# Where the buffers live in SBUF: TensorE's operands stacked from the low end, raw weights, h and small pieces from the high end

## The chip, the cores and the metric

One core of a Trainium2 chip runs the whole program. The metric is the device time of one execution in microseconds (us). Runs of one kernel repeat within some tenths of a microsecond here; of a change in this kernel a measurement can tell about 0.2%.

## What is computed

One layer of a streaming encoder on 256 tokens of width 2048, in float32:

```python
h = x + 0.5 * swiglu(rms_norm(x), ffn1...)             # d_ff = 5632
u = rms_norm(h); z_pool, q, k, v = split(u @ w_in)     # w_in 2048 x 4096
y_pool = pool_mixer(z_pool)                            # 4 groups, windows 2, 4, 8, 16
y_attn = chunk_attention(q, k, v)                      # 8 heads of 128, chunk 64
gates = sigmoid(u @ w_branch_gate + b)                 # 2048 x 4096
merged = gates_pool * (y_pool @ w_br_pool) + gates_attn * (y_attn @ w_br_attn)
h = h + merged @ w_out
h = h + 0.5 * swiglu(rms_norm(h), ffn2...)
h = h + sigmoid(rms_norm(h) @ w_ple_gate) * (p @ w_ple)
```

The inputs hold 444 MB of data that the DMAs move, nearly all of it weights that are read once.

## The kernel before

**Weights in two words.** Every weight tile, 512 rows by 512 columns (128 partitions x 4 x 512, 8 KB per partition), comes as float32 by one DMA into a raw buffer (`wraw`). ScalarE rounds it to a float32r high word `whi` (L155), VectorE subtracts for the low word `wlo` (L163). TensorE's left-hand operands (the activations, turned so that tokens are columns) are split in the same way, by `split` (L112 to L114). A product then has three passes per 128 rows: low activation x `whi` (L198), high activation x `whi` (L200), high activation x `wlo` (L205). In each, the 128x128 activation tile is loaded into the array and 512 columns of the weight tile stream past it. Each of the three lines issues 2,884 matmuls of that shape.

**Items.** The program is a flat list of items (one weight tile and its matmuls), which `stream` (L172) writes out: for item i it issues the DMAs of up to five items ahead (as rooms are free), the high word of item i + 2, the low word of item i + 1 and the matmuls of item i. Engine queues are in the order in which this writes them (`manual_schedule`). Four of the six raw buffers are not interchangeable: `ROOMS` (L38) gives one each to the tags wa, wb, wc, and three to wr.

**Blocks.** The FFN products and the last gate use `block` (L375), which makes 2x2 tiles of four weights with seven products instead of eight: seven items of 12 matmuls, and two or four "rest" items of 24 matmuls on the inner tiles beyond the first 1024 (L423). Three sums of raw weights are made in the raw buffers by VectorE (L413, L417, L420) and one by an accumulating DMA of GpSimd (L414). An FFN runs in parts of 4, 4 and 3 column blocks (`FFN_PARTS`, L37); each part has its up/gate blocks, whose left-hand operands are the normed `u` tiles (`uah`, `ual`, `ush`, `usl`, `uhi`, `ulo`), and two down blocks, whose left-hand operands are the `hid` tiles. A down block has two rest items per side in parts 1 and 2 and one per side in part 3.

**Mixer.** Between the FFNs, `mixer` (L750) computes the input projection, attention, pooling, the gates (`w_branch_gate`), and per 512 columns `w_br_pool` and `w_br_attn` of 8 tiles' depth, in two items each: the first on `ypool` (kept in the room wc) or on spare `u` tiles, the second on `ypoolhi`/`ypoollo` or `yattnhi`/`yattnlo` of the pool `mix`. Of the four `merged` operands that `w_out` reads, the first two lie in the rooms wa and wb, the other two (`mergedl`) in `mix`. `v` and `z` lie in wa and wb too.

**Homes.** A pool is a run of addresses, the same on all partitions; pools are stacked in the order in which they are opened. Homes in KB of a partition, as built:

| what | before | changed |
|---|---|---|
| `ident` and other constants (pool const) | 16 to 17 | 16 to 17 |
| raw weights, tag wr (3) | 17 to 41 | 176 to 200 |
| `whi` (3) | 41 to 65 | 17 to 41 |
| `wlo` (2) | 65 to 81 | 41 to 57 |
| rooms wa, wb, wc (raw weights; `merged`, `v`, `z`, `ypool`) | 81 to 105 | 200 to 224 |
| `h` (2) | 105 to 121 | 149 to 165 |
| `u` tiles (pool act) | 121 to 165 | 57 to 101 |
| small pieces, statistics (pool work) | 165 to 176 | 165 to 176 |
| pools hid, mix, late, opened and closed on the way | 176 to 224 | 101 to 149 |

Of the kernel before, what the change touches and what calls it, by code (L numbers as in the profile page):

```python
# [10 lines left out]
F32 = mybir.dt.float32  # L11
F32R = mybir.dt.float32r
# [4 lines left out]
P = 128  # L17
SEQ = 256
NT = SEQ // P
D = 2048  # L20
# [13 lines left out]
NB = 512  # L34
KB = 4
KW = 2
FFN_PARTS = (4, 4, 3)  # L37
ROOMS = {"wa": 1, "wb": 1, "wc": 1, "wr": 3}  # L38
# [3 lines left out]
def hybrid_block(ctx: ExitStack, tc: tile.TileContext, a: dict, out: bass.AP):  # L42
    nc = tc.nc

    const = ctx.enter_context(tc.tile_pool(name="const", bufs=1))
    wpool = ctx.enter_context(tc.tile_pool(name="wpool", bufs=1))
    act = ctx.enter_context(tc.tile_pool(name="act", bufs=1))
    work = ctx.enter_context(tc.tile_pool(name="work", bufs=1))
    ps_acc = ctx.enter_context(tc.tile_pool(name="ps_acc", bufs=6, space=bass.MemoryType.PSUM))
    ps_tp = ctx.enter_context(tc.tile_pool(name="ps_tp", bufs=2, space=bass.MemoryType.PSUM))  # L50

# [34 lines left out]
    def piece_tile(name):  # L86
        return work.tile([P, NB], F32, tag="piece", name=name, bufs=PIECES)
# [11 lines left out]
    def later(steps, task):  # L99
        waiting.append([steps, task])  # L100
# [18 lines left out]
    def room(tag, name):  # L119
        assert free[tag] > 0, tag  # L120
        free[tag] -= 1
        return wpool.tile([P, KB, NB], F32, tag=tag, name=name, bufs=ROOMS[tag])

    class Weight:

# [5 lines left out]
        def load(self):  # L131
            self.raw = room(self.tag, "wraw")
            at_once = KW if self.halves else self.nk
            for k in range(0, self.nk, at_once):
                ks = slice(k, k + at_once)
                nc.sync.dma_start(self.raw[:, ks, :], self.src[:, ks, :])
# [109 lines left out]
    def product(w, lhs, n0, done, k0=0, nks=(KB,) * (D // P // KB), halves=False):  # L246

        got = []

        def banks():  # L250
            if not got:
                got.extend(acc_tile("acc") for _ in range(NT))
            return got

        items, kt = [], k0
        for i, nk in enumerate(nks):
            end = i == len(nks) - 1
            items.append(Item(
                Weight(w, kt, n0, nk, halves=halves and not i),
                both(banks, lambda i=i: lhs()[i], done if end else None, last=end),  # L260
            ))
            kt += nk
        return items
# [204 lines left out]
        nc.vector.tensor_tensor(r, r, s, op=ALU.mult)  # L468
        return r

    h = [act.tile([P, D], F32, tag=f"h{t}", name=f"h{t}") for t in range(NT)]

    def token_tiles(b):

# [8 lines left out]
    def turn(dst, src, t):  # L483

        tp = turned(src)
        if isinstance(dst, Half) and not dst.b:
            f = dst.place(t)
            nc.scalar.copy(out=f, in_=tp)
            dst.take(t, f)
        else:  # L490
            dst.take(t, tp)
# [120 lines left out]
    def hooked(items, before):  # L612

        mm = items[0].mm

        def new(it):
            before()
            mm(it)

        items[0].mm = new  # L620
        return items
# [128 lines left out]
    def mixer(norm, following, flat, carry):  # L750
# [7 lines left out]

        def begin():
            mix = m_["mix"] = inner.enter_context(tc.tile_pool(name="mix", bufs=1))  # L760
            yp = wpool.tile([P, 2, KB, SEQ], F32R, tag="wc", name="ypool", bufs=ROOMS["wc"])
            free["wc"] -= 1
            y["pool"] = [
                Operand(None, "", 1, missing=KB, tiles=(yp[:, 0], yp[:, 1])),
                Operand(mix, "ypool", 1, missing=KB),
            ]

            yh, yl = (s[:, 2:4, :].rearrange("p b (k s) -> p (b k) s", s=SEQ) for s in norm.spare)
            y["attn"] = [
                Operand(None, "", 1, missing=KB, tiles=(yh, yl)),  # L770
                Operand(mix, "yattn", 1, missing=KB),
            ]
# [50 lines left out]
        for blk in range(2):  # L823
            for which, c0 in (("q", POOL_W), ("k", POOL_W + 1024)):
                items = product(w_in, lhs, c0 + blk * NB, heads(which))
                if first:
                    hooked(items, begin)
                    first = False
                flat += items


        def plain(c0, tag, name, then):
            got = []
            items = []
            for blk in range(2):
                def done(accs, blk=blk):
                    if not got:
                        both_ = room(tag, name)
                        got.extend(both_[:, 2 * t:2 * t + 2, :] for t in range(NT))
                    for t in range(NT):  # L840
                        nc.scalar.activation(got[t][:, blk, :], accs[t], AF.Copy, scale=norm.r[t])
                    if blk:
                        then([g.rearrange("p b n -> p (b n)") for g in got])
                items += product(w_in, lhs, c0 + blk * NB, done)
            return items
# [139 lines left out]
        merged = []  # L985
        for n in range(D // NB):
            g = [[], []]
            for br in range(2):
                c0 = br * D + n * NB

                def bias_row(c0=c0, g=g):
                    bb = m_["mix"].tile([P, NB], F32, tag="bb", name="bb", bufs=1)
                    nc.gpsimd.dma_start(
                        bb, a["b_branch_gate"][0, c0:c0 + NB].partition_broadcast(P)
                    )
                    m_["bb"] = bb

                def done(accs, br=br, g=g):
                    for t in range(NT):
                        s = piece_tile("g")  # L1000
                        nc.vector.scalar_tensor_tensor(
                            s, accs[t], norm.r[t], m_["bb"], op0=ALU.mult, op1=ALU.add
                        )
                        nc.scalar.activation(s, s, AF.Sigmoid)
                        g[br].append(s)

                flat += hooked(product(w_gate, lhs, c0, done), bias_row)

            def done_pool(accs, g=g, n=n):
                for t in range(NT):  # L1010
                    nc.vector.tensor_tensor(g[0][t], accs[t], g[0][t], op=ALU.mult)
                if n == D // NB - 1:
                    free["wc"] += 1

            def done_attn(accs, g=g, n=n):
                if n < 2:
                    tag = ("wa", "wb")[n]
                    free[tag] -= 1
                    both_ = wpool.tile([P, 2, KB, SEQ], F32R, tag=tag, name="merged",
                                       bufs=ROOMS[tag])  # L1020
                    dst = Operand(None, "", 1, tiles=(both_[:, 0], both_[:, 1]))
                else:
                    dst = Operand(m_["mix"], "", 1, tiles=[
                        m_["mix"].tile([P, KB, SEQ], F32R, tag="mid", name="mergedl", bufs=4)
                        for _ in range(2)
                    ])
                for t in range(NT):
                    nc.vector.tensor_tensor(g[1][t], accs[t], g[1][t], op=ALU.mult)
                    nc.vector.tensor_tensor(g[0][t], g[0][t], g[1][t], op=ALU.add)
                    later(2 + t, lambda t=t, dst=dst: turn(dst, g[0][t], t))  # L1030
                merged.append(dst)

            flat += product(a["w_br_pool"][0], lambda: y["pool"], n * NB, done_pool, nks=(KB, KB))
            flat += product(a["w_br_attn"][0], lambda: y["attn"], n * NB, done_attn, nks=(KB, KB))

        for n in range(D // NB):
# [186 lines left out]
```

## Time and profile before

| | us |
|---|---|
| median of 3 runs (2165.03 to 2165.77) | 2165.55 |
| the profiled execution | 2166.04 |
| its span, first to last instruction | 2164.0 |
| TensorE busy in it | 2088.7 (97%) |
| TensorE's weight loads busy | 1693.5 (78%) |
| VectorE busy | 1666.5 (77%) |
| ScalarE busy | 1156.0 (53%) |
| GpSimd busy | 66.0 (3%) |

Engines are named as in the rows: PE is TensorE's matmuls, PEld its weight loads (here the loads of the activation tile), DVE is VectorE, ACT ScalarE, POOL GpSimd, SP the engine that issues most DMAs. A row names line, engine, operation, output<-inputs and shapes. Matmuls are pipelined: the record of one (about 390 ns) overlaps the next, so the distance of two starts tells the pace. The granted clock is a share of TensorE's full 2.4 GHz.

### The profile page before, as it was taken

Reading aid. Unit: us, or ns where it says so; the run is one execution under the profiler, and the core shown is the slowest. Engines: PE = TensorE matmul, PEld = TensorE weight load, DVE = VectorE, ACT = ScalarE, POOL = GpSimd, SP = SyncE. Lnnn points to the kernel's source line nnn. Section 1 sums busy time; section 2 is a strip of 40 time slices with the busy share of each in tenths; the row PEclk is TensorE's granted clock in tenths of the full one; section 3 lists DMA queues with packets and bytes.
Section 4 is the critical chain, followed back from the end, with each engine's and each line's share of the span. In section 5 each row is a group of like instructions: output and inputs, shape, how many; then the busy total and the mean of one; then the engine's idle time right before and its main releaser. Section 6 shows DMA issues by size and latency. Waiting matters only on the chain. (4 is left out here: it accounts for less than half of the span.)

```text
span 2164.0 us, 22839 instructions
## 1 busy us (share of the span) xinstructions
PE 2088.7 (97%) x9206; PEld 1693.5 (78%) x9206; DVE 1666.5 (77%) x1211; ACT 1156.0 (53%) x1004; POOL 66.0 (3%) x89
## 2 busy tenths in 40 slices
PE   7999999999999899999999999999999999999798
PEld 5878888788887678887888887878788788877576
DVE  5788888888888766554555557898888888888787
ACT  3655456554565743453434356655455555555564
POOL 0000000000000000000000000000000000000000
PEclk9999999999999999999999999999999999999899
DMA  6577577657765655554666556776677567756564
GB/s 224 181 239 227 179 249 243 208 179 259 242 195 171 207 188 192 189 168 159 198 195 195 195 170 192 261 222 204 205 262 230 179 221 255 224 175 215 171 183 156
DMA packets 222441, 444.02 MB, mean 205 GB/s; under 512 B 7480, under 2 KB 7552, under 8 KB 222336
## 3 DMA queue, kind: packets, MB, share of 16 engines
q1 hardware_dynamic: 201968, 400.59, 53.0%
q0 software_dynamic: 20368, 41.98, 10.1%
q8 instruction: 72, 1.18, 0.2%
q14 instruction: 33, 0.27, 0.0%
HBM read 440.44 MB, written 2.10 MB: 204 GB/s over the span
## 5 line engine op out<-in xcount | busy, mean ns | idle before, releaser
L163 DVE TENSOR_TENSOR wlo<-wraw,whi 128x2048 fp32r<-128x2048 f32 (+1 forms) x486 | 1100.8, 2274 | 292.3 <-PE acc L205 144.8
L155 ACT CAST whi<-wraw 128x2048 fp32r<-128x2048 f32 (+1 forms) x486 | 921.0, 1901 | 684.8 <-PE acc L200 185.3
L198 PE MATMUL acc<-whi,ulo 128*128 128x512 f32 x288 | 114.6, 398 | 0.0
L200 PE MATMUL acc<-whi,uhi 128*128 128x512 f32 x288 | 113.3, 393 | 0.0
L198 PE MATMUL acc<-whi,ual 128*128 128x512 f32 x216 | 89.1, 412 | 5.5 <-ACT whi L155 5.5
L200 PE MATMUL acc<-whi,uah 128*128 128x512 f32 x216 | 87.1, 403 | 0.0
L417 DVE TENSOR_TENSOR wraw<-wraw 128x2048 f32<-128x2048 f32 x35 | 80.2, 2292 | 1.2
L413 DVE TENSOR_TENSOR wraw<-wraw 128x2048 f32<-128x2048 f32 x35 | 80.2, 2292 | 1.2
L420 DVE TENSOR_TENSOR wraw<-wraw 128x2048 f32<-128x2048 f32 x35 | 80.0, 2286 | 0.0
L205 PE MATMUL acc<-wlo,uhi 128*128 128x512 f32 x288 | 77.2, 390 | 0.0
L198 PE MATMUL acce<-whi,ulo 128*128 128x512 f32 x184 | 73.2, 398 | 0.0
L198 PE MATMUL accd<-whi,ulo 128*128 128x512 f32 x184 | 72.0, 391 | 0.8 <-ACT p L597 0.8
L200 PE MATMUL acce<-whi,uhi 128*128 128x512 f32 x184 | 71.8, 390 | 0.0
L198 PE MATMUL accb<-whi,usl 128*128 128x512 f32 x184 | 71.8, 390 | 0.0
L198 PE MATMUL acca<-whi,ulo 128*128 128x512 f32 x184 | 71.7, 390 | 0.0
L200 PE MATMUL accd<-whi,uhi 128*128 128x512 f32 x184 | 71.7, 390 | 0.0
L200 PE MATMUL acca<-whi,uhi 128*128 128x512 f32 x184 | 71.7, 390 | 0.0
L200 PE MATMUL accb<-whi,ush 128*128 128x512 f32 x184 | 71.7, 390 | 0.0
L198 PE MATMUL accb<-whi,ual 128*128 128x512 f32 x184 | 71.7, 390 | 0.0
L200 PE MATMUL accb<-whi,uah 128*128 128x512 f32 x184 | 71.6, 389 | 0.0
L198 PE MATMUL accb<-whi,ulo 128*128 128x512 f32 x184 | 71.6, 389 | 0.0
L200 PE MATMUL accb<-whi,uhi 128*128 128x512 f32 x184 | 71.6, 389 | 0.0
(328 smaller groups left out, 4237.6 us busy)
## 6 DMA issues: line engine op xcount, KB each, us to landing
wraw<-in_ffn_w_up_dram SPq DMA_DIRECT2D x88, 1024.0 KB, 7.1
wraw<-in_ffn_w_down_dram SPq DMA_DIRECT2D x88, 1024.0 KB, 9.3
wraw<-in_ffn_w_gate_dram SPq DMA_DIRECT2D x87, 1024.0 KB, 8.8
wraw<-in_w_in_dram SPq DMA_DIRECT2D x32, 1024.0 KB, 5.4
wraw<-in_w_branch_gate_dram SPq DMA_DIRECT2D x32, 1024.0 KB, 5.4
wraw<-in_ffn_w_gate_dram POOLq DMA_DIRECT2D x21, 1024.0 KB, 12.3
wraw<-in_w_out_dram SPq DMA_DIRECT2D x16, 1024.0 KB, 5.0
wraw<-in_w_ple_gate_dram SPq DMA_DIRECT2D x16, 1024.0 KB, 7.6
```

Source lines behind the costliest of these rows:

```text
L155: nc.scalar.copy(out=self.hi[:, ks, :], in_=w.raw[:, ks, :])
L163: nc.vector.tensor_tensor(out=self.lo[:, ks, :], in0=w.raw[:, ks, :], in1=self.hi[:, ks, :].bitcast(F32), op=ALU.subtract,)
L198: nc.tensor.matmul(acc, xl, wh[:, k, :], start=start and k == 0, stop=False, skip_group_check=True)
L200: nc.tensor.matmul(acc, xh, wh[:, k, :], start=False, stop=False, skip_group_check=True)
L205: nc.tensor.matmul(acc, xh, wl[:, k, :], start=False, stop=last and k == len(forms) - 1, skip_group_check=True)
L413: tt(b11.raw, b11.raw, b12.raw, op=ALU.add)
L417: tt(b11.raw, b11.raw, b22.raw, op=ALU.add)
L420: tt(b21.raw, b21.raw, b11.raw, op=ALU.add)
```

## The change

Two pools are opened on the other side of SBUF (`side="right"`, stacked from the high end): a new one, `rawpool`, from which all raw weight rooms come, the operands that borrow such a room (`ypool`, `merged`; `v` and `z` by way of `room`) among them, and `work`, with the small pieces, which takes in `h` as well. Sizes and numbers of buffers stay. On every engine the same instructions stand in the same order with the same waits as before; only addresses differ.

```diff
--- before.py
+++ after.py
@@ -43,9 +43,11 @@
     nc = tc.nc
 
     const = ctx.enter_context(tc.tile_pool(name="const", bufs=1))
+
     wpool = ctx.enter_context(tc.tile_pool(name="wpool", bufs=1))
     act = ctx.enter_context(tc.tile_pool(name="act", bufs=1))
-    work = ctx.enter_context(tc.tile_pool(name="work", bufs=1))
+    rawpool = ctx.enter_context(tc.tile_pool(name="rawpool", bufs=1, side="right"))
+    work = ctx.enter_context(tc.tile_pool(name="work", bufs=1, side="right"))
     ps_acc = ctx.enter_context(tc.tile_pool(name="ps_acc", bufs=6, space=bass.MemoryType.PSUM))
     ps_tp = ctx.enter_context(tc.tile_pool(name="ps_tp", bufs=2, space=bass.MemoryType.PSUM))
 
@@ -119,7 +121,7 @@
     def room(tag, name):
         assert free[tag] > 0, tag
         free[tag] -= 1
-        return wpool.tile([P, KB, NB], F32, tag=tag, name=name, bufs=ROOMS[tag])
+        return rawpool.tile([P, KB, NB], F32, tag=tag, name=name, bufs=ROOMS[tag])
 
     class Weight:
 
@@ -468,7 +470,7 @@
         nc.vector.tensor_tensor(r, r, s, op=ALU.mult)
         return r
 
-    h = [act.tile([P, D], F32, tag=f"h{t}", name=f"h{t}") for t in range(NT)]
+    h = [work.tile([P, D], F32, tag=f"h{t}", name=f"h{t}") for t in range(NT)]
 
     def token_tiles(b):
 
@@ -758,7 +760,7 @@
 
         def begin():
             mix = m_["mix"] = inner.enter_context(tc.tile_pool(name="mix", bufs=1))
-            yp = wpool.tile([P, 2, KB, SEQ], F32R, tag="wc", name="ypool", bufs=ROOMS["wc"])
+            yp = rawpool.tile([P, 2, KB, SEQ], F32R, tag="wc", name="ypool", bufs=ROOMS["wc"])
             free["wc"] -= 1
             y["pool"] = [
                 Operand(None, "", 1, missing=KB, tiles=(yp[:, 0], yp[:, 1])),
@@ -1016,7 +1018,7 @@
                 if n < 2:
                     tag = ("wa", "wb")[n]
                     free[tag] -= 1
-                    both_ = wpool.tile([P, 2, KB, SEQ], F32R, tag=tag, name="merged",
+                    both_ = rawpool.tile([P, 2, KB, SEQ], F32R, tag=tag, name="merged",
                                        bufs=ROOMS[tag])
                     dst = Operand(None, "", 1, tiles=(both_[:, 0], both_[:, 1]))
                 else:
```

## Rows read from the trace of the kernel before

**Rows 1.** The page's head and busy times: us, share of the span, instructions.

```profile
span 2164.0 us, 22839 instructions
...
PE 2088.7 (97%) x9206; PEld 1693.5 (78%) x9206; DVE 1666.5 (77%) x1211; ACT 1156.0 (53%) x1004; POOL 66.0 (3%) x89
```

**Rows 2.** Groups of TensorE's instructions: busy us, mean ns of one | idle before.

```profile
L200 PE MATMUL accb<-whi,uah 128*128 128x512 f32 x184 | 71.6, 389 | 0.0
...
L200 PE MATMUL accb<-whi,hidah 128*128 128x512 f32 x96 | 37.9, 395 | 0.0
...
L198 PE MATMUL acc<-whi,mergedl 128*128 128x512 f32 x64 | 25.3, 395 | 0.0
```

**Rows 3.** TensorE's timeline in `w_br_pool`: start us, length us, instruction.

```profile
1208.12 0.39 PE L198 MATMUL acc<-whi,ypool 128*128 128x512 f32 x1
...
1213.57 0.39 PE L198 MATMUL acc<-whi,ypoollo 128*128 128x512 f32 x1
...
1219.16 0.40 PE L198 MATMUL acc<-whi,usl 128*128 128x512 f32 x1
```

**Rows 4.** TensorE's timeline in `w_out`.

```profile
1276.45 0.40 PE L198 MATMUL acc<-whi,merged 128*128 128x512 f32 x1
...
1285.62 0.39 PE L198 MATMUL acc<-whi,merged 128*128 128x512 f32 x1
...
1288.35 0.39 PE L198 MATMUL acc<-whi,mergedl 128*128 128x512 f32 x1
...
1299.55 0.40 PE L198 MATMUL acc<-whi,merged 128*128 128x512 f32 x1
```

**Rows 5.** Stretches: length; busy us (instructions) of PE, PEld, DVE, ACT, POOL; clock, DMA share, GB/s.

```profile
208.00:286.00 78.00, 78.00 (x339) 62.37 (x338) 67.86 (x45) 39.96 (x23) 2.20 (x2) 1.00 0.65 216
294.00:456.00 162.00, 159.17 (x708) 129.91 (x707) 141.17 (x88) 94.93 (x72) 3.83 (x3) 1.00 0.66 217
678.00:752.00 74.00, 65.76 (x290) 50.64 (x290) 61.03 (x45) 47.38 (x61) 1.91 (x3) 1.00 0.49 157
1230.00:1323.00 93.00, 93.00 (x420) 75.68 (x419) 54.44 (x42) 47.70 (x64) 0.42 (x1) 1.00 0.57 193
1970.00:2053.00 83.00, 68.98 (x288) 53.24 (x287) 65.84 (x52) 46.83 (x59) 1.28 (x1) 0.92 0.46 151
```

**Rows 6.** Waits of weight loads, 208 to 286 us: us in total, times, longest.

```profile
PEld acce L205 <- DVE wlo L163: 0.7, 2, 0.4
```

**Rows 7.** Waits of TensorE in the last parts, 678:752, then 1970:2053.

```profile
PE tp L480 <- ACT gained L529: 3.4, 3, 2.1
...
PE tp L480 <- ACT sq L539: 6.3, 3, 4.8
```

**Rows 8.** Groups of VectorE and ScalarE, shapes apart.

```profile
L114 DVE TENSOR_TENSOR hidsl<-blocks,hidsh 128x512 fp32r<-128x512 f32 x19 | 13.2, 693 | 13.1 <-ACT hidsh L113 13.1
...
L114 DVE TENSOR_TENSOR usl<-blocks,ush 128x512 fp32r<-128x512 f32 x9 | 6.2, 693 | 6.2 <-ACT ush L113 6.2
...
L113 ACT CAST hidsh<-blocks 128x512 fp32r<-128x512 f32 x19 | 11.8, 622 | 29.3 <-DVE blocks L355 11.2 <-DVE blocks L350 8.6 <-DVE blocks L352 8.2
...
L113 ACT CAST ush<-blocks 128x512 fp32r<-128x512 f32 x9 | 5.6, 620 | 13.0 <-DVE blocks L350 4.9 <-DVE blocks L352 4.1 <-DVE blocks L355 4.1
```

**Rows 9.** DMA issues: KB each, median us from issue to landing.

```profile
bb<-in_b_branch_gate_dram POOLq DMA_DIRECT2D x8, 256.0 KB, 3.5
```

**Rows 10.** Groups of TensorE's transposes.

```profile
L480 PE MATMUL tp<-ident,qraw 128*128 128x128 f32 x32 | 4.8, 272 | 0.0
...
L904 PE MATMUL tp<-ident,sc 128*128 128x128 f32 x24 | 3.9, 271 | 0.0
```

**Rows 11.** Two waits on TensorE's timeline; one stretch, columns as in group 5.

```profile
721.75 0.44 PE L480 MATMUL tp<-ident,h 128*128 128x128 f32 x2 [2.10 <-ACT gained L529]
...
2010.14 1.11 PE L480 MATMUL tp<-ident,h 128*128 128x128 f32 x4 [4.76 <-ACT sq L539]
...
2008.20:2015.00 6.80, 4.86 (x14) 3.99 (x15) 6.76 (x7) 5.57 (x9) 0.00 (x0) 0.50 1.06 236
```

## The prediction

> **What bounds the kernel now.** I read the page first, then TensorE's groups, then TensorE's timeline at places where only the home of an operand differs, then a table by stage. On the page TensorE is busy for 2088.7 of 2164.0 us, VectorE 77%, ScalarE 53% [rows 1]: what counts is the pace of the 8,652 matmuls of the three passes (L198, L200, L205) and the few places where TensorE waits.
>
> That pace has two values. The mean record of a pass is 389 ns where its left-hand operand (the 128x128 tile held in the array; the weight tile streams past it) is a `u` tile, and 395 ns where it is a `hid` or `mergedl` tile [rows 2], one group of each kind; same shapes, same lines, same weight homes. Records overlap, so the price is taken between starts. One instance of `w_br_pool` [rows 3]: the 24 matmuls on `ypool` (home 97 to 105 KB) run from 1208.12 to 1213.57, 5.45 us or 227.1 ns each; the next 24, on `ypoollo`/`ypoolhi` (home from 175.6 KB), from 1213.57 to 1219.16, 5.59 us or 232.9 ns each. Two halves of one product, back to back, from one stream of weights; what differs is the home. `w_out` says the same [rows 4]: 12 matmuls on `merged` (wb, 89 to 97 KB) take 2.73 us, 227.5 ns each; the 48 on `mergedl` that follow (192 KB and up) take 11.20 us, 233.3 ns each. So I read: **a left-hand operand at 175.6 KB and above costs about 6 ns per matmul against one at 165 KB and below** (5.8 in both pairs, taken as 6 below). The step lies somewhere in the 11 KB between; why it is there the trace doesn't show.
>
> **The change part by part.** Instructions, their order and their waits are the same on every engine; so only the speed of accesses can move, and whatever waits follow from it.
>
> *The `hid`, `mix` and `late` pools come down* from 175.6 to 224 KB, to 101 to 149 KB. By the code, a down block has seven items of 12 matmuls and rest items of 24, four in parts 1 and 2 and two in part 3: 84 + 96 = 180 matmuls, or 132; a part has two blocks: 360 or 264. Gross: four full parts at 360 x 6 ns = 2.16 us, two last parts at 264 x 6 = 1.58, 192 on `ypoolhi/lo` and `yattnhi/lo` 1.15, 192 on `mergedl` 1.15, 48 on `p` 0.3 (24 more at the start, on the tile that `beside` lends, are left out): 8.6 + 3.2 + 2.6 = 14.4 us.
>
> What of it reaches the end? In a full down stretch TensorE is never idle (78.00 of 78) and VectorE works 67.86 [rows 5]; at 76 us it would be 89% busy. The cover is thin: VectorE is already the last to release a weight load once per block, 0.7 us in two waits that today lie under the matmul before [rows 6]. A faster TensorE meets that wait. In the up/gate stretch, which already runs at the low pace, VectorE is 87% busy and TensorE idles 2.83 of 162 us [rows 5]; that share of 78 us is 1.36. Bounds on what a full part keeps: 2.16, and 0.8. I take 1.75, nearer the upper end, because the wait already seen is small: 7.0 us from four.
>
> In the last parts TensorE has idle time, 8.2 of 74 us and 14.0 of 83 [rows 5], and it ends mostly by ScalarE, which squares and turns the new `h` (`gained` L529, `sq` L539) [rows 7], and whose work this change does not shorten. A faster matmul there mostly arrives earlier at a wait. Bounds 0 and 1.58 each; I take 0.3, near zero: 0.6 us from two. In the mixer and the PLE stage TensorE is full while VectorE has room (93.00 and 54.44 of 93 in `w_out`, [rows 5]): 2.6 in full. Together 10.2 us.
>
> *`ypool` and two of four `merged` go the other way.* Their rooms wa, wb, wc move with the raw weights from 81 to 105 KB up to 200 to 224 KB, although TensorE reads them as left-hand operands. 96 matmuls on `ypool` x 5.8 = 0.56 us lost. Of the 192 on `merged` only some have anything to lose: the 48 from 1276.45 to 1288.35 take 11.90 us, two groups of four transposes among them, the first 36 of them 9.17 or 255 ns each, and only the last 12 run at 227.5 [rows 4]: between transposes the low home does not give its low pace. Bounds 0 and 192 x 5.8 = 1.1; I take 0.35. Lost: 0.9 us.
>
> *Raw weights, `h` and small pieces go up.* VectorE and ScalarE show no step: L114 takes 693 ns from and to high homes (`hidsl`) and 693 with a low output (`usl`), L113 takes 622 and 620 [rows 8]. So the passes over raw weights (L155, L163, the sums) are costed at nothing. The nearest row that says otherwise is the 2 ns of L113, 0.3%; on VectorE's 1666.5 us that would be 5 us, and TensorE waits for it only in a small share of the time (2.83 of 162 us in the up/gate stretch): bounds 0 to 1 us. `h` at 149 to 165 KB stays below the lowest slow home. Loads now land high; the 256 KB loads that did so before, `bb`, took 3.5 us from issue to landing [rows 9], no sign of a slow one, and raw weights are issued up to five items (of 12 or 24 matmuls, 2.7 us and more) ahead: 0, at worst 1 us.
>
> Sum: 10.2 - 0.9 = **9.3 us faster**. The profiled execution took 2166.04 us (span 2164.0), 0.5 above the median of 2165.55; against the median this is **2156.3**.
>
> Here the Trainium skill speaks against the change. On the page "SBUF — State Buffer", section "SBUF: two separate sides", TensorE never waits on another engine or on a DMA for SBUF, and no region of a partition is named as slower. By that, moving homes is worth nothing.
>
> **Rivals.**
>
> *No effect, 2165.5.* The slow pace would belong to the work around the matmuls and not to the home. For it: the transposes show no step, 271 ns with `sc` (210 KB) held in the array, 272 with `qraw` (165 to 175 KB) [rows 10]. By the skill's rule just named, this would be the outcome. Against it: the two pairs of [rows 3, 4], where the pace turns within one product and turns back; a transpose streams 128 columns, not 512, and may hide what a pass shows. A last form of it is that only half the gain survives the waits of VectorE: -4 us, within 0.2%. Chance of either 0.13.
>
> *More than forecast, about 2149.* If what makes the pace slow after an interruption [rows 4] also comes from TensorE's reads sharing a region with what others write, taking the raw weights and pieces away helps the `u` stretches too: that is at most the 6 ns on those that follow one; with one in ten of some 6,000 (an estimate from the places where transposes stand) 3.6 us. The bounds above (full parts keep all, 1.6 more; last parts 0.5 each; `merged` loses nothing, 0.35) add the rest of some 7 in all. Chance 0.1.
>
> *Slower, about 2184.* The streamed weights, `whi`, move from 41 to 65 KB down to 17 to 41 KB, where the trace has TensorE stream only `ident`. If that region, shared with the `const` tiles, had the same 6 ns for streamed operands, 5,768 matmuls of L198 and L200 would lose 34.6 us; with four fifths reaching the end, 28, less 9 is +19. It decides from about a third of these matmuls on (9.3 / 0.8 / 6 ns = 1,900). Against it: `ident` streams from there at 271 to 272 ns per transpose [rows 10], whichever tile is held, and nothing in the passes distinguishes the three homes that `whi` rotates over. Chance 0.05.
>
> *The clock.* In FFN2's last part and just after, the granted clock stands at 0.50 (the 1.2 GHz level) for 6.8 us, behind a TensorE wait of 4.76 us [rows 11]; there are three such pieces from 2008 us on. A wait of 2.10 us in FFN1's last part has none behind it [rows 11]. A piece costs up to half its length, 3.4 us. Earlier arrivals may lengthen such a wait into one piece more or shift one away: +-3.4 within the forecast case.
>
> **How the numbers follow.** Forecast case 0.72: 2156.3, by its own bounds (parts 4 x 0.8 to 2.16, last parts 0 to 1.58, rooms, one clock piece either way) 2150.5 to 2162. More than forecast 0.1, none or half 0.13, slower 0.05. The range 2148.5 to 2162.5 takes in the forecast and most of the larger gain. A measurement of this kernel can tell about 0.2%, 4.3 us: faster than 2161.2 has 0.80 (the two faster cases less 0.02 at the forecast's upper end), within 0.2% 0.15, slower 0.05.
>
> **What would show it.** Right: passes on `hid`, `mergedl`, `yattn` and `p` tiles at 389 to 391 ns instead of 395; `ypool` and `merged` the other way; the four full down stretches about 1.8 us shorter each with small `wlo` waits that were not there; the last parts nearly as long as before. Wrong: `hid` passes still at 395 ns (the home is not the cause); `u` passes above 391 (the new homes of `whi` cost); longer passes of VectorE or ScalarE over raw weights; or a fourth piece at 0.50 of the clock.

## The result, and the profile after

The changed kernel takes **2153.28 us** (median of 6 runs, 2152.08 to 2155.28) where the kernel before took 2164.64 on the same chips: ratio 0.9948, 95% interval 0.9935 to 0.9961. It is faster, by 11.4 us; the forecast was 2156.3, range 2148.5 to 2162.5. Runs of one kernel spread here over 2 to 3 us, and not over the tenths of a microsecond named above; the gain is several times that.

The page of the changed kernel, as in [rows 1]:

```profile
span 2151.7 us, 22839 instructions
...
PE 2073.4 (96%) x9206; PEld 1693.7 (79%) x9206; DVE 1665.5 (77%) x1211; ACT 1155.8 (54%) x1004; POOL 66.0 (3%) x89
```

TensorE's busy time is down by 15.3 us; the others' moves by less than 1.1. Lines after L48 have shifted by 2 (L198, L200, L205 are now L200, L202, L207; L163 is L165). Its groups of TensorE's matmuls, as in [rows 2], with `ypool`, which lies in a borrowed room:

```profile
L202 PE MATMUL accb<-whi,uah 128*128 128x512 f32 x184 | 71.6, 389 | 0.0
...
L202 PE MATMUL accb<-whi,hidah 128*128 128x512 f32 x96 | 37.4, 390 | 0.0
...
L200 PE MATMUL acc<-whi,mergedl 128*128 128x512 f32 x64 | 24.9, 389 | 0.0
...
L202 PE MATMUL acc<-whi,ypool 128*128 128x512 f32 x32 | 12.5, 390 | 0.0
```

`hidah` and `mergedl` went from 395 to 390 and 389 ns, as forecast. `ypool`, whose home is now at 216 to 224 KB, stayed at 390, and that was not forecast. In the kernel before its row is the same:

```profile
L200 PE MATMUL acc<-whi,ypool 128*128 128x512 f32 x32 | 12.5, 390 | 0.0
```

TensorE's timeline of the `w_br_pool` of [rows 3] shows both in one product:

```profile
1200.56 0.39 PE L200 MATMUL acc<-whi,ypool 128*128 128x512 f32 x1
...
1206.00 0.39 PE L200 MATMUL acc<-whi,ypoollo 128*128 128x512 f32 x1
...
1211.44 0.39 PE L200 MATMUL acc<-whi,usl 128*128 128x512 f32 x1
```

Both halves take 5.44 us for 24 matmuls, 226.7 ns each: the high one and the low one alike.

Where the 12.3 us of the two profiled spans went, from the starts of the same instructions in both traces: the four full FFN parts give 1.90, 1.89, 1.89 and 1.88 (sum 7.56); the last part of FFN1 is 0.09 longer, that of FFN2 0.61; the last two of the four pairs of `w_br_pool` and `w_br_attn` give 0.79, `w_out` 1.47, the last gate with `p` 0.39; the start gives 0.73; the mixer between 997 and 1102 us, with the first two pairs in it, gives 2.36; the 60 us behind FFN2 take back 0.51, the rest (six stretches) 0.2 net. Stretches of the changed kernel, columns as in group 5:

```profile
207.50:285.50 78.00, 77.73 (x345) 63.70 (x345) 69.25 (x45) 40.19 (x23) 2.55 (x2) 1.00 0.67 224
...
673.30:746.30 73.00, 64.78 (x285) 51.00 (x284) 60.69 (x44) 46.22 (x59) 1.30 (x1) 0.98 0.50 159
...
1957.00:2040.00 83.00, 68.53 (x285) 53.24 (x284) 65.08 (x52) 46.00 (x59) 1.28 (x1) 0.92 0.46 149
```

The full down stretch now holds 345 matmul records in 78 us instead of 339, and VectorE works 69.25 us in it instead of 67.86 [rows 5]; TensorE, never idle there before, now idles 0.27 us: VectorE all but keeps up. In FFN1's last part the clock's mean fell from 1.00 to 0.98, in FFN2's it stayed at 0.92.

The 2.36 us are mostly clock: of the four pairs the last three give 0.38 us each, the first 1.92. A stretch of the kernel before inside that first pair, and its counterpart in the changed one (same columns, the clock third from the end):

```profile
1011.50:1014.90 3.40, 3.40 (x9) 2.66 (x9) 0.97 (x2) 0.76 (x2) 0.00 (x0) 0.50 0.04 14
```

```profile
1006.60:1010.20 3.60, 3.60 (x18) 2.92 (x17) 1.00 (x3) 0.86 (x2) 0.00 (x0) 1.00 0.04 15
```

The kernel before has a 3.41 us piece at 0.50 (1.2 GHz) there, 9 matmuls in it, and the changed one has none: half the piece is 1.7 us, and the first pair is 1.5 ahead of the others. Two experiments below bear this out: with the slow pace on `hid` in both, the one without this piece (128 bytes) gains 1.90 us between these points, the one with it (64 bytes) 0.19.

### The profile page after: what moved, and what is told of

Its sections match the earlier page's. It is cut to its first block, busy times and chain, and to the rows that moved or that the text cites. A ratio compares the mean times of both kernels' runs of the same rounds, so it can differ in the third digit from the quotient of the medians.

```text
span 2151.7 us, 22839 instructions
## 1 busy us (share of the span) xinstructions
PE 2073.4 (96%) x9206; PEld 1693.7 (79%) x9206; DVE 1665.5 (77%) x1211; ACT 1155.8 (54%) x1004; POOL 66.0 (3%) x89
## 5 line engine op out<-in xcount | busy, mean ns | idle before, releaser
L165 DVE TENSOR_TENSOR wlo<-wraw,whi 128x2048 fp32r<-128x2048 f32 (+1 forms) x486 | 1099.8, 2273 | 287.7 <-PE acc L207 143.4
L157 ACT CAST whi<-wraw 128x2048 fp32r<-128x2048 f32 (+1 forms) x486 | 921.1, 1901 | 676.1 <-PE acc L202 184.1
L200 PE MATMUL acc<-whi,ulo 128*128 128x512 f32 x288 | 114.7, 398 | 0.0
L202 PE MATMUL acc<-whi,uhi 128*128 128x512 f32 x288 | 113.0, 392 | 0.0
L200 PE MATMUL acc<-whi,ual 128*128 128x512 f32 x216 | 89.1, 413 | 5.7 <-ACT whi L157 5.7
L202 PE MATMUL acc<-whi,uah 128*128 128x512 f32 x216 | 86.7, 401 | 0.0
L207 PE MATMUL acc<-wlo,uhi 128*128 128x512 f32 x288 | 77.1, 389 | 0.0
L200 PE MATMUL acce<-whi,ulo 128*128 128x512 f32 x184 | 73.2, 398 | 0.0
L200 PE MATMUL accd<-whi,ulo 128*128 128x512 f32 x184 | 71.9, 391 | 0.8 <-ACT p L599 0.8
L202 PE MATMUL acce<-whi,uhi 128*128 128x512 f32 x184 | 71.8, 390 | 0.0
L200 PE MATMUL accb<-whi,usl 128*128 128x512 f32 x184 | 71.7, 390 | 0.0
L202 PE MATMUL accd<-whi,uhi 128*128 128x512 f32 x184 | 71.6, 389 | 0.0
L202 PE MATMUL accb<-whi,ush 128*128 128x512 f32 x184 | 71.6, 389 | 0.0
L200 PE MATMUL accb<-whi,ual 128*128 128x512 f32 x184 | 71.6, 389 | 0.0
L202 PE MATMUL accb<-whi,uah 128*128 128x512 f32 x184 | 71.6, 389 | 0.0
L200 PE MATMUL acca<-whi,ulo 128*128 128x512 f32 x184 | 71.6, 389 | 0.0
L202 PE MATMUL acca<-whi,uhi 128*128 128x512 f32 x184 | 71.6, 389 | 0.0
L200 PE MATMUL accb<-whi,ulo 128*128 128x512 f32 x184 | 71.6, 389 | 0.0
L202 PE MATMUL accb<-whi,uhi 128*128 128x512 f32 x184 | 71.6, 389 | 0.0
```

What stands on the lines that cost most here:

```text
L157: nc.scalar.copy(out=self.hi[:, ks, :], in_=w.raw[:, ks, :])
L165: nc.vector.tensor_tensor(out=self.lo[:, ks, :], in0=w.raw[:, ks, :], in1=self.hi[:, ks, :].bitcast(F32), op=ALU.subtract,)
L200: nc.tensor.matmul(acc, xl, wh[:, k, :], start=start and k == 0, stop=False, skip_group_check=True)
L202: nc.tensor.matmul(acc, xh, wh[:, k, :], start=False, stop=False, skip_group_check=True)
L207: nc.tensor.matmul(acc, xh, wl[:, k, :], start=False, stop=last and k == len(forms) - 1, skip_group_check=True)
```

## The experiments

That `ypool` and `merged` kept their pace above 200 KB spoke against the region that the forecast named. The homes, written out to the byte, gave a rival. Before, every tile that the three passes read starts at a remainder of 480 modulo 512, but for the tiles of `hid`, `mix` and `late`, at 128 (modulo 64: 32 and 0). In the changed kernel all of them have 480, the rooms too. **Region** (the theory on record) against **start**: what counts is where the held and the streamed tile start, as remainders. Since held pieces step by 512 bytes and streamed ones by 2,048, the remainder by 512 is the same for all pieces of a tile. "Pace" below is the mean distance from start to start of a kind's matmuls, without the gaps above 262 ns. All experiments compute the whole layer; they add unused bytes or shift tiles. Experiments 1, 2 and 10 have several runs, the others one each; what they are used for is the pace in the trace, and a time of one run is given as it came.

**1. The kernel before, 32 unused bytes below the pool `hid`,** which stays high:

```diff
         stream(flat, lambda first: load_x(norms[0], first))
+        work.tile([P, 8], F32, tag="pad", name="pad")
```

> The kernel before with an unused 32-byte tile at the end of the pool work: the pools hid, mix and late start 32 bytes higher, still at 175.7 KB and above, and at 32 instead of 0 modulo 64 bytes. Theory A (a held operand that starts at 0 modulo 64 bytes is slow, one at 32 modulo 64 fast, wherever it lies): hid and mergedl passes at 389 to 391 ns, starts 227 ns apart, time like the changed kernel, 2152 to 2156 us. Theory B (the step is the region, 175 KB and above): 395 ns, 233 ns apart, 2163.6 to 2165.8 us. Theory C (fast only where held operand and weight tile start at the same offset modulo 512 bytes, 480 for both in every fast case so far; here 160): as B.

2154.2 us (2152.99 to 2155.83), ratio 0.9954, interval 0.9937 to 0.9971: 32 bytes give about what the change gave. The pace of `hid`, `mergedl`, `yattn` and `p` is 229.1 ns, neither the 227 nor the 233 of the three cases on record. TensorE's groups of this kernel:

```profile
L200 PE MATMUL accb<-whi,uah 128*128 128x512 f32 x184 | 71.6, 389 | 0.0
...
L200 PE MATMUL accb<-whi,hidah 128*128 128x512 f32 x96 | 37.6, 392 | 0.0
```

The region as the whole cause falls; it could still own the last 2 ns.

**2. The changed kernel, 32 unused bytes below `hid`,** which stays low (the same line, with `act.tile`).

> The changed kernel with an unused 32-byte tile at the end of the pool act: hid, mix and late start at 0 instead of 32 modulo 64 bytes, in the low region (101 to 149 KB). A: hid, mergedl, yattn and p passes back at 395 ns, 233 ns apart, time back to 2162 to 2166 us. B: 389 to 391 ns, 2152 to 2156 us. C (offset 0 modulo 512 against 480): as A.

2163.53 us (2162.07 to 2166.22), ratio 0.9992, interval 0.9983 to 1.0002: the gain is gone, with every region as in the changed kernel. Its group shows the old 395 ns, its pace is 233.2:

```profile
L202 PE MATMUL accb<-whi,hidah 128*128 128x512 f32 x96 | 37.9, 395 | 0.0
```

**3 and 4. Tables of starts in one run.** In the first, each `u` tile of the changed kernel is 32 bytes longer, so that the held tiles start at 480, 0, 32, 64, 96, 128, 160 and 192 modulo 512, with the weights at 480; in the second the weight tiles are longer, and `hid` has 32 unused bytes below it as well. Of the first, the function and none of its uses:

```diff
+    def long_tile(pool, n, m, tag, bufs=1):
+        more = 8 if tag[0] == "u" else 0
+        t = pool.tile([P, n * m + more], F32R, tag=tag, name=tag, bufs=bufs)
+        return t[:, :n * m].rearrange("p (n m) -> p n m", n=n)
...
```

> The changed kernel with every u tile 32 bytes longer than its contents, so that their starts step through 480 (uah), 0 (ual), 32 (ush), 64 (usl), 96 and 128 (uhi), 160 and 192 (ulo) modulo 512 bytes; weight tiles stay at 480, hid at 224. A: uah and ush 227 ns from start to start, ual and usl 233, uhi and ulo half and half, hid 227; about 2,500 matmuls slow, gross 14 us, some 11 at the end: 2161 to 2167 us. B: all at 227, 2152 to 2156 us. C: only uah at 227, all other u and hid tiles at 233, 2180 us or more. A step of another period would show as another pattern over the tiles.

2177.49 us, between the cases on record (2161 to 2167, and 2180 or more). `uah`, which still starts where the weights do, has lost its pace as well: 395 ns, 230.7 from start to start.

```profile
L202 PE MATMUL accb<-whi,uah 128*128 128x512 f32 x184 | 72.6, 395 | 0.0
...
L202 PE MATMUL accb<-whi,hidah 128*128 128x512 f32 x96 | 37.4, 390 | 0.0
```

Its passes on `whi` alternate with passes on `ual`, 32 bytes off; its four passes on `wlo` follow one another and are slow too (230.2). So slow matmuls seem to slow matched ones behind them; the fifth experiment has the clean case. That spoils this design for single starts, where good and bad tiles alternate every 4 to 12 matmuls. `hid`, in its own long stretches, is readable: it has slid to 224 modulo 512, 256 from the weights, and runs at 227.5.

> The changed kernel with whi and wlo tiles 32 bytes longer than their contents, so that the streamed weight tiles start at 480, 0 and 32 (whi) and 64 and 96 (wlo) modulo 512 bytes; the u tiles are at 0 modulo 64, hid at 32 modulo 64. A as it stands (the held operand alone): all u passes at 233 ns, all hid passes at 227, whichever weight buffer streams; about 5,900 matmuls slow, 2175 to 2185 us. A relative (both at the same offset modulo 64 is fast): the pace follows the weight buffer, u fast where it starts at 0 modulo 64, hid fast where at 32; about half of all slow, 2165 to 2178 us. B: all at 227, 2152 to 2156 us.

2189.08 us, again outside the cases; all distances lie between 229.5 and 233.7 ns. Inconclusive, for the same reason.

**5 to 7. Smaller shifts.** Pairs of `uhi`/`ulo` start 16 and 48 bytes into lengthened tiles, then 4 and 8, with `OFFSETS` in elements; then the weights start 16 bytes into theirs.

```diff
+    OFFSETS, turns = (4, 12), [0]
...
+        t = pool.tile([P, n * m + (16 if tag[0] == "u" else 0)], F32R, tag=tag, name=tag, bufs=bufs)
+        return t[:, at:at + n * m].rearrange("p (n m) -> p n m", n=n)
...
```

> The changed kernel with the two pairs uhi/ulo moved inside longer tiles so that one pair starts at 48 and the other at 16 modulo 64 bytes; every other operand and all weight tiles stay at 32. If the rule is a period of 64 bytes with one good place: both pairs at 233 ns from start to start, about 3,900 matmuls slow, gross 23 us, 2168 to 2176 us. If 0 modulo 64 is the one bad place: both at 227, 2152 to 2156. If a place exists that is better than 32: below 226 ns in one of the pairs, down to 213 (512 columns at one per cycle of 2.4 GHz).

> As the run on 16 and 48, with the pairs uhi/ulo at 36 and 40 modulo 64 bytes, 4 and 8 bytes above the good place. One good place only: both at 233 ns, 2168 to 2176 us. One bad place only (0): both at 227, 2152 to 2156. A cost of starts inside a 16-byte line would show as more than 233.

> The changed kernel with whi and wlo moved 16 bytes up inside longer tiles, so that all streamed weight tiles start at 48 modulo 64 bytes; all held operands stay at 32. If the streamed tile obeys the same rule as the held one and 32 is the one good place: all passes at about 233 ns, 2180 to 2192 us. If only 0 is bad: 227, 2152 to 2156. Below 226 would be a better place.

2163.42, 2167.46 and 2188.93 us; the first two times lie in none of their cases. The pair meant to be 16 bytes ahead modulo 64 has a median of 227 and a mean of 229.1 ns, the pair 16 behind 233.2; 4 and 8 bytes 232.5 and 232.1. With the weights shifted every pass slows, to 232.4 on the mean. Because each tile also grew, the distances modulo 512 are mixtures (16, 144, 112 and 240 in the first), and good and bad tiles alternate again: these three show that shifts of 4 and 8 bytes are not free, and give no clean value for one distance. They do show two things. `hid`, which has slid to a distance of 256 in the first two, runs at 227.5 and 227.4 there, as in the third experiment. And the slow pace outlasts its cause: the items of 12 passes on `ual`/`uah` and `usl`/`ush`, all matched, that come right behind an unmatched item have 228.8 ns in their first four passes, 229.1 in the next four and 226.7 in the last four (230.2, 228.3 and 227.0 with 4 and 8 bytes); in the changed kernel the same items have 226.8, 226.8 and 226.7.

**8. The changed kernel, 32 unused bytes below everything** (in `const`), so that weights, `u` and `hid` all start at 0 modulo 512, while the rooms stay at 480.

> The changed kernel with an unused 32-byte tile at the end of the pool const: whi, wlo, u, hid, mix and late tiles all start at 0 modulo 64 bytes; ypool and merged, in the raw rooms, stay at 32. If both operands at the same offset were what counts, 227 ns and 2152 to 2156 us. If each of the two has to be at 32: all passes at 232 to 234 ns, 2185 to 2195 us.

2152.04 us in one run. The groups turn around:

```profile
L202 PE MATMUL accb<-whi,hidah 128*128 128x512 f32 x96 | 37.4, 390 | 0.0
...
L202 PE MATMUL acc<-whi,merged 128*128 128x512 f32 x64 | 25.3, 395 | 0.0
...
L202 PE MATMUL acc<-whi,ypool 128*128 128x512 f32 x32 | 12.7, 396 | 0.0
```

`hid` at 0 with weights at 0 is fast, `ypool` and `merged` at 480, untouched, have become slow (233.1), because the weights moved away from them. No start is good by itself; **what counts is the distance of the two starts.** Until here a remainder by 64 explained every readable run but for the 229 of the first. The last four were chosen for that rest.

**9 to 12. Which distance, and is there a rest of the region?** The changed kernel with 64, 192 and 128 unused bytes in `act`, and the kernel before with 352 in `work`, which puts the high `hid` at 480 modulo 512, level with the weights. Each is the one line of the first experiment, with 16, 48, 32 and 88 elements.

> The changed kernel with 64 unused bytes at the end of the pool act: hid, mix and late start 64 bytes higher, in the low region still; held and streamed tiles still have the same start modulo 64 bytes, but differ by 64 modulo 128. If only the remainder by 64 counts and what was left of the slow pace with the 32 bytes added to the kernel before (229 ns from start to start) came from the high region: hid and mergedl 227 to 227.5 ns, 390 ns in the groups, 2153 us. If the 229 came from a distance that is no multiple of 128: about 229 ns, 392 in the groups, 2154 to 2157 us. If the page of 512 bytes or the region were what counts in full: 233 ns, 2163 us.

> The kernel before with 352 unused bytes at the end of the pool work: hid, mix and late stay above 175 KB, and start at the same place modulo 512 as the weights. If only distance counts, the passes on hid, mergedl, yattn and p run at 227 ns (390 in the groups) although they lie high, and the time is that of the changed kernel, 2152 to 2155 us. If the high region keeps a rest of its own: 229 ns, 392 in the groups, 2154 to 2157 us. If the region counts in full: 233 ns, 2164 us.

> The changed kernel with 192 unused bytes at the end of act: in the low region, the distance of held and streamed starts is 192 modulo 512, the one that the kernel before had with 32 bytes added. Distance modulo 128 or 512 as the cause of the rest: hid and mergedl 229 ns, 392 in the groups, 2154 to 2157 us. Region as its cause: 227 to 227.5 ns, 390 in the groups, 2153 us.

> The changed kernel with 128 unused bytes at the end of act: a distance of 128 modulo 512. If a finer relation by 128 bytes exists, this run has hid and mergedl at 227 ns where distances of 64 and 192 have 229; if by 256 or 512, 229 ns as these; if only 64 counts, 227 to 227.5 ns in all three, 2153 us.

Results for 64, 352, 192 and 128 bytes: 2164.48; **2153.87** (5 runs, 2153.28 to 2157.43, ratio 0.9951, interval 0.9938 to 0.9965); 2156.31; 2164.37 us. The groups of each, first 64 bytes:

```profile
L202 PE MATMUL accb<-whi,hidah 128*128 128x512 f32 x96 | 37.8, 394 | 0.0
```

The kernel before with 352 bytes, its page, then its groups:

```profile
PE 2073.7 (96%) x9206; PEld 1694.8 (79%) x9206; DVE 1665.4 (77%) x1211; ACT 1155.8 (54%) x1004; POOL 66.0 (3%) x89
```

```profile
L200 PE MATMUL accb<-whi,hidah 128*128 128x512 f32 x96 | 37.4, 390 | 0.0
...
L198 PE MATMUL acc<-whi,mergedl 128*128 128x512 f32 x64 | 24.9, 389 | 0.0
```

192 bytes, then 128:

```profile
L202 PE MATMUL accb<-whi,hidah 128*128 128x512 f32 x96 | 37.6, 392 | 0.0
```

```profile
L202 PE MATMUL accb<-whi,hidah 128*128 128x512 f32 x96 | 37.8, 394 | 0.0
```

Two things fall here. The remainder by 64: 64 and 128 bytes keep it and lose the whole gain, which the text on record for 64 bytes had given to the 512-byte page or the region, and which none of the cases for 128 bytes had (227 to 229 ns; it has 232.9). And any rest of the region: 192 bytes give the 229.1 ns in the low region that the first experiment had, at the same distance, in the high one; and the kernel before, every pool where it was, reaches the full pace and the changed kernel's time with 352 unused bytes. What stands, from stretches in which one distance holds for long:

| start of held minus streamed tile, modulo 512 | run | pace, ns |
|---|---|---|
| 0 | changed; 352 bytes in the kernel before (`hid` high) | 227.4; 227.3 |
| 256 | third, fifth and sixth experiment, `hid` | 227.5; 227.5; 227.4 |
| 192 | first (high); 192 bytes (low) | 229.1; 229.1 |
| 32, 64, 128 | 32, 64, 128 bytes in the changed kernel | 233.2, 233.3, 232.9 |
| 160 | the kernel before | 233.4 |
| 480 | rooms of the eighth | 233.1 |

Why a distance costs 6 ns is not shown: no row tells what holds a load or a stream up, and the records of the weight loads are 188 to 191 ns at either pace. No version clearly beats the changed kernel: the one with 352 bytes and the eighth have its time within what the runs can tell.

## Why the prediction was right, and where it was wrong

The time, the direction and the size came out; the cause did not. That the change worked all the same was luck: it moved `work`, whose small statistics tiles had shifted `hid` by the odd 160 bytes, to the other end, and the rooms there happen to start at 480 too; the forecast asked for neither.

**The step that failed** is the reading "a left-hand operand at 175.6 KB and above costs about 6 ns per matmul against one at 165 KB and below". The 6 ns were right (233.4 against 227.4), and so was the list of tiles that pay them. Put in place of the region by the runs: the distance of the two starts, 160 bytes modulo 512 before, 0 after. In the kernel before the two readings could not be told apart, since the only tiles with another remainder were the ones above 175.6 KB; the forecast saw that the step lay "somewhere in the 11 KB between" and didn't ask what else changed there. The two chosen pairs of operands differed in both.

**Rooms, 0.9 lost:** wrong, by the failed step. `ypool` has 227.5 ns before and 227.2 after, `merged` 229.6 and 228.5. Nothing was lost. The 255 ns that the forecast read for `merged` between transposes were misread as well: they include 0.7 us of the transposes themselves, and the 229.6 leaves such gaps out.

**Four full parts, 7.0:** 7.56. The term of VectorE's cover, 1.75 of 2.16 each, came out at 1.89. The wait that it was to meet grew a little. Waits of weight loads in the changed kernel's first down stretch (207.5 to 285.5 us), as in [rows 6]:

```profile
PEld acce L207 <- DVE wlo L165: 1.1, 2, 0.6
```

That is 1.1 us for 0.7, and the 0.27 us that TensorE now idles there are about what the 1.89 lack of 2.16.

**Last parts, 0.6 gained:** 0.70 lost. A faster matmul did arrive at the same waits. The changed kernel's, FFN1 and then FFN2, as in [rows 7]:

```profile
PE tp L482 <- ACT gained L531: 3.5, 3, 2.1
PE tp L482 <- ACT sq L541: 3.4, 3, 1.9
```

```profile
PE tp L482 <- ACT sq L541: 6.4, 3, 4.9
```

They are as long as before, and TensorE pays for clock besides. Three stretches of the changed kernel, then one of the kernel before, columns as in group 5:

```profile
1996.90:2000.31 3.41, 3.41 (x10) 2.90 (x11) 3.41 (x3) 3.41 (x4) 0.00 (x0) 0.50 1.13 212
2010.50:2020.74 10.24, 7.90 (x18) 5.73 (x19) 5.23 (x7) 5.31 (x6) 0.00 (x0) 0.50 0.00 0
716.90:720.31 3.41, 3.41 (x11) 2.83 (x12) 3.41 (x3) 2.35 (x3) 0.00 (x0) 0.50 0.49 85
```

```profile
2025.30:2032.10 6.80, 3.94 (x9) 3.14 (x10) 4.32 (x5) 2.54 (x3) 0.00 (x0) 0.50 0.00 0
```

The piece at 716.90 is new, behind FFN1's waits, where the kernel before had 1.00; TensorE works all through it, which costs about what 264 faster matmuls gain. In FFN2, 3.41 and 10.24 us at 0.50 stand in place of 6.83 and 6.83 (the other of them in [rows 11]): the same length, but TensorE works 11.3 us in them where it worked 8.8, and the 2.5 us more at half the clock cost about 1.2 (an estimate: half of them).

**Mixer and PLE, 2.6 in full:** about 3.4: 0.8 for the first two pairs without the clock piece, 0.79 for the other two, `w_out` 1.47, the last gate with `p` 0.39. Kept in full, as forecast, and undersized: `mergedl` went from 233.3 to 226.7 ns, 6.6 instead of 6, and the passes behind each slow stretch gained some 0.04 us as well.

**Clock, +-3.4:** one piece gone in the mixer (about 1.5 us gained), one come in FFN1, one more at the start (6.83 us from 10.33 on, in which TensorE works 4.2 us as before), others shifted behind FFN2. The forecast had named a further piece as a sign of being wrong; it came, and the one that went outweighs it. On the spans the gain is 12.3 for 9.3: rooms +0.9, full parts +0.56, last parts -1.3, mixer and PLE +0.85, and +2.0 from what the forecast gave no term (the start 0.73, the clock in the mixer 1.55, behind FFN2 -0.51, the rest 0.23). The medians differ by 11.4. So the good number is in part terms that cancel: what was lost in the last parts came back in the clock and the rooms. The bounds of the forecast's terms, all taken at one end, would also give more than its 2150.5 to 2162: 2148 to 2165.

**Passes and loads at nothing:** right. L165 has a mean of 2273 ns, before 2274; L157 1901 in both.

**The rivals.** "No effect" didn't come. Its evidence, the transposes, stands, but says nothing on the cause: from start to start they take 108 ns with `sc`, 0 bytes modulo 512 from `ident`, and 108 with `qraw`, 352 from it, so no step by distance shows with 128 columns. And the rule of the Trainium skill beside it (page "SBUF — State Buffer", section "SBUF: two separate sides") names no region as slower: on regions these runs agree with it, and it has nothing on the distance of two starts that they show. The rival "slower", a slow home for `whi`, fell: `uah` is at 389 ns as before. "More than forecast" has its time a little further off (2149) than the forecast has, but its share of the cause, `u` stretches helped by the raw weights' leaving, shows no more than 0.2 ns on `uah` (227.5 to 227.3), and the slow pace "after an interruption" that it built on was the misread 255 ns.

## What to carry to other kernels

When two groups of matmuls of one shape differ by 2 or 3% in pace, write down both operands' start addresses to the byte, not only where they live: here 352 unused bytes did what the whole change did. Pad pools so that the held and the streamed tiles start at the same remainder modulo 512, and look again after every new small tile, since 32 bytes between the two homes undo it. And a test that alternates good and bad cases within some ten matmuls shows neither, because the slow pace outlasts its cause by about eight; give each case a stretch of its own.

## What the runs showed of the hardware

A 128x512 float32r pass took 227 ns from start to start where held and streamed tiles started 0 or 256 bytes apart modulo 512, 229 at 192, and 233 at 32, 64, 128, 160 and 480. The relation is between the two operands: `ypool`, at the same home, turned from 227 to 233 when the weights moved away from it. The slow pace persists: behind an unmatched item, matched passes took 229 to 230 ns at first and were back at 227 in the last four of twelve (fifth and sixth experiment); with bad tiles every few matmuls they ran at 230.7 (third). Transposes of 128 columns took 108 ns at a distance of 0 and of 352. Still open: why 192 lies between, whether distances below 32 differ (16, and 144 as well, had a median of 227 in a mixed run, 4 had one of 232), and what holds the slow passes up.
